# Modulation of a diffusion step in units of 1024 columns on one Trainium2 core

## The chip, the core and the metric

One core of one Trainium2 chip runs the whole program. The metric is the device time of one execution in microseconds; lower is better. The engines are TensorE (PE; PEld is its weight load), VectorE (DVE), ScalarE (ACT), GpSimd (POOL) and SyncE (SP), which here issues almost all DMAs, in the order of the program.

## The reference, cut to what matters

The model has two layers, 128 context and 256 latent tokens, and a width D of 1024. Each layer begins with a modulation that depends on nothing but two conditioning vectors (one for context, one for latent tokens):

```python
def adaln(cond, w, b):
    m = jax.nn.silu(cond) @ w + b          # w: (1024, 6 * 1024)
    return jnp.split(m[..., None, :], 6, axis=-1)
# shift1, scale1, gate1, shift2, scale2, gate2
h = layer_norm(x) * (1 + scale1) + shift1
...
x = layer_norm(alpha * x + gate1 * mix)
x = layer_norm(alpha * x + gate2 * peer(layer_norm(x) * (1 + scale2) + shift2))
```

So the modulation weights are 2 x 1024 x 6144 floats, 50 MB, each read once and multiplied with two vectors. `mix` is a token mixer (state-space scan, neighbourhood attention, grouped-query attention) behind one combined input projection; `peer` looks 16 experts per head and token up out of 16384 by two score lists of 128 keys.

## The kernel before, in words

**Weights.** Every weight goes through one ring of eight buffers `w` of 512 KB (`wst`, N_RAW = 8), filled by SyncE in program order; a load is issued once the buffer that was filled eight loads earlier has been read. A block of the input projection is split into a high and a low part (`split`, lines 218 to 225: ScalarE casts `uh`, VectorE or, for the first N_FIRST = 3 blocks, GpSimd subtracts to `ul`; three buffers of each), and multiplied in 24 matmuls of 384 columns (`proj3`, lines 361 to 371).

**Modulation.** `adaln_unit` (line 253) makes 256 columns of one of the six parts of one layer. It loads two `w` buffers, multiplies each of the eight k-slices with the conditioning `condT` (128 x 32, of which two columns are used), k-slice k in column group k % 4 of the array, so that PSUM holds four partial sums below each other (line 259). ScalarE copies them to `modp` (line 261). The second half of the unit, run when the next unit has begun, multiplies `modp` with a 0/1 table `sel` in two matmuls of two columns (line 265), which adds the four partial sums and puts the columns on partitions; two ScalarE operations add the bias and write `mcol` (line 268). There are 48 units, in the list `todo`.

```python
for k in range(KD):
    q = k % 4
    T.matmul(ps[32 * q:32 * q + 32, :256], condT[:, k, :], w[k], start=(k < 4), stop=(k >= 4), tile_position=(0, 32 * q))
...
for a in range(2):
    T.matmul(pt[:, 2 * a:2 * a + 2], mp[:, a * 128:(a + 1) * 128], sel, start=True, stop=True)
```

**Where the units run.** Eight run at the start (line 438): `cond_prep` makes `condT` and the bias columns `bmT`; then for each pair of k-slices two units (a shift and a scale) and behind them the transposes of the normalised tokens (line 441), modulated by ScalarE (line 444, `hraw`) and split into `hh` and `hl`. In the mixer, `blocks` (line 373) runs one unit behind every second weight block, up to N_FILL = (16, 8) by layer. At the third token tile of the output projection N_AD = 4 more run (line 1110; in layer 1 all that are left, two). In the routing of layer 0, `tick` (line 1187) runs one behind each of the query blocks 6 to 15. Routing is a loop over 16 query blocks of TensorE, each followed on VectorE by top-16 searches (`best`), with a long piece (`pairs`) behind blocks 7 and 15.

A tile scheduler orders the instructions of each engine at build time; engines then run them in that order and wait on semaphores.

Of the kernel before, what the change touches and what calls it, by code (L numbers as in the profile page):

```python
# [19 lines left out]
KD = 8  # L20
# [20 lines left out]
N_FILL = (16, 8)  # L41
N_AD = (4, 4)
# [11 lines left out]
R_AD = 4  # L54
# [55 lines left out]

CAND = []
# [44 lines left out]
def hybrid_step(ctx: ExitStack, tc: tile.TileContext, A, O):  # L156
# [71 lines left out]
    fill_ps, fill_n, first = [None], [0], [0]  # L228


    def cond_prep(sp, ps1):
        cond = mk(sp, [16, 128], "cond")
        dma(out=cond[0:8, :], in_=A["c_ctx"].rearrange("(k p) -> k p", p=128))
        dma(out=cond[8:16, :], in_=A["c"].rearrange("o (k p) -> (o k) p", p=128))
        V.memset(condT, 0.0)
        ps = mk(ps1, [128, 512], "pt")
        T.transpose(ps[:, :16], cond, ident[:16, :16])
        th = mk(sp, [128, 16], "cth")
        S.activation(th, ps[:, :16], AF.Tanh, scale=0.5)
        cc = mk(sp, [128, 16], "cc")  # L240
        S.activation(cc, ps[:, :16], AF.Copy, scale=0.5)
        V.scalar_tensor_tensor(condT[:, :, 0:2].rearrange("p k c -> p c k"), th.rearrange("p (c k) -> p c k", c=2), 1.0,
                               cc.rearrange("p (c k) -> p c k", c=2), op0=ALU.add, op1=ALU.mult)
        for l in range(DEPTH):
            bm = mk(sp, [48, 128], "bm", bufs=2)
            dma(out=bm, in_=A["b_mod"][l].rearrange("(k p) -> k p", p=128))
            ps = mk(ps1, [128, 512], "pt")
            T.transpose(ps[:, :48], bm, ident[:48, :48])
            V.tensor_copy(bmT[:, l], ps[:, :48])
            for part in (1, 4):  # L250
                V.tensor_scalar(bmT[:, l, part * KD:(part + 1) * KD], bmT[:, l, part * KD:(part + 1) * KD], 1.0, None, op0=ALU.add)

    def adaln_unit(l, part, hb, ps1, tags):

        w = load_k(A["w_mod"][l, part * 4 + hb])
        ps = mk(ps1, [128, 512], tags[0])
        for k in range(KD):
            q = k % 4
            T.matmul(ps[32 * q:32 * q + 32, :256], condT[:, k, :], w[k], start=(k < 4), stop=(k >= 4), tile_position=(0, 32 * q))
        mp = mk(outer, [128, 256], "modp", bufs=2)  # L260
        S.copy(mp, ps[:, :256])
        yield
        pt = mk(ps1, [128, 512], tags[1])
        for a in range(2):
            T.matmul(pt[:, 2 * a:2 * a + 2], mp[:, a * 128:(a + 1) * 128], sel, start=True, stop=True)
        c = part * KD + 2 * hb
        for a in range(2):
            S.activation(mcol[:, l, part, 2 * hb + a, :], pt[:, 2 * a:2 * a + 2], AF.Identity, bias=bmT[:, l, c + a:c + a + 1])

    todo = []  # L270
    for l, ps in ((0, (0, 1)), (0, (2,)), (0, (3, 4)), (1, (0, 1)), (0, (5,)), (1, (2,)), (1, (3, 4)), (1, (5,))):
        todo += [(l, part, hb) for hb in range(4) for part in ps]
    begun = []

    def adaln(n, ps1, tags, flush=False):

        for _ in range(min(n, len(todo))):
            u = adaln_unit(*todo.pop(0), ps1, tags)
# [94 lines left out]
    def blocks(src, b0, n):  # L373

        for j in range(n):
            yield load_w(src[b0 + j])
            if j % 2 and fill_n[0] > 0:
# [40 lines left out]
    def mixer(l, stack, right, ps1):  # L418
# [4 lines left out]
        with ExitStack() as sc0:  # L423
# [6 lines left out]
            if l == 0:  # L430
# [19 lines left out]
        fill_ps[0], fill_n[0], first[0] = ps1, N_FILL[l], N_FIRST  # L450
# [573 lines left out]
    def peer(l, mg, right, mps, ps1):  # L1024
# [162 lines left out]
        def tick(b):  # L1187
            u_steps(U_R.get(b, 0))
            if l == 0 and b >= N_WQ + R_AD:
# [124 lines left out]
def blocked(inputs):  # L1314
# [15 lines left out]
    d["w_mod"] = cut(d["w_mod"], 4, 256)  # L1330
# [28 lines left out]
```

## Time and profile before

| | us |
|---|---|
| three runs, median | 2998.48 |
| lowest, highest | 2995.82, 3007.12 |
| the profiled execution | 3004.09 |
| its span | 3002.3 |
| PE busy in the span | 2855.6 (95%) |
| DVE busy | 2309.1 (77%) |
| ACT busy | 1396.8 (47%) |

By time the span is: start until about 50 us; mixer of layer 0 until 486; output projection until 543; routing until 715; gate table and experts until about 1545; the same for layer 1, mixer until 1988, routing until 2192, experts until the end. Busy time is a share of the span only; whether a piece of work costs time is read from the waits of its stage.

### The profile page before, as it was taken

Reading aid. Unit: us, or ns where it says so; the run is one execution under the profiler, and the core shown is the slowest. Engines: PE = TensorE matmul, PEld = TensorE weight load, DVE = VectorE, ACT = ScalarE, POOL = GpSimd, SP = SyncE. Lnnn points to the kernel's source line nnn. Section 1 sums busy time; section 2 is a strip of 40 time slices with the busy share of each in tenths; the row PEclk is TensorE's granted clock in tenths of the full one; section 3 lists DMA queues with packets and bytes.
Section 4 is the critical chain, followed back from the end, with each engine's and each line's share of the span. In section 5 each row is a group of like instructions: output and inputs, shape, how many; then the busy total and the mean of one; then the engine's idle time right before and its main releaser. Section 6 shows DMA issues by size and latency. Waiting matters only on the chain.

```text
span 3002.3 us, 48719 instructions
## 1 busy us (share of the span) xinstructions
PE 2855.6 (95%) x17953; PEld 2479.3 (83%) x17953; DVE 2309.1 (77%) x4888; ACT 1396.8 (47%) x2861; POOL 824.8 (27%) x566
## 2 busy tenths in 40 slices
PE   7999999999889999999969999999987999999996
PEld 5888889877779999998858888898876999999985
DVE  3645654599669999998976466547986999999988
ACT  4544543225754444444445455432178544444443
POOL 1000000002334455554540000000033444555554
PEclk9999999999889999999979999999999999999998
DMA  6454322565999999999934432233569999999994
GB/s 246 151 159 146 95 72 87 182 223 167 316 364 408 391 392 396 393 391 369 379 97 144 127 93 74 85 111 113 156 217 371 418 395 392 394 391 394 393 364 166
DMA packets 299328, 767.09 MB, mean 256 GB/s; under 512 B 42770, under 2 KB 113874, under 8 KB 299090
## 3 DMA queue, kind: packets, MB, share of 16 engines
q1 hardware_dynamic: 225362, 495.51, 46.2%
q0 software_dynamic: 73728, 268.47, 23.5%
q8 instruction: 141, 2.31, 0.3%
q14 instruction: 97, 0.79, 0.1%
HBM read 726.92 MB, written 36.96 MB: 254 GB/s over the span
## 4 chain that ended last, share of the span: by engine, by line
PE 74%; DVE 11%; DMA 6%; ACT 4%; issue 4%; POOL 1%; SPq 0%; POOLq 0%; ACTq 0%; DVEq 0%
PE hp L1167 6%; PE out L1243 6%; PE hp L1169 6%; PE out L1245 6%; PE hp L1168 6%; PE out L1244 6%; PE pp L368 5%; PE pp L369 5%; PE pp L370 5%; PE hp L1164 4%; DMA w<-in_peer_uT 3%; PE pp L947 2%; ACT ol L1004 2%; DVE vl L224 2%; DVE tn L1073 2%
## 5 line engine op out<-in xcount | busy, mean ns | idle before, releaser
L1057 POOL DMA_INDIRECT prow<-in_peer_u,ei x256 | 363.1, 1418 | 763.1 <-DVE prow L1062 523.5
L1068 POOL DMA_INDIRECT prow<-in_peer_v,ei x256 | 382.4, 1494 | 350.1 <-DVE tn L1073 308.6
L222 ACT CAST vh<-w 128x1024 fp32r<-128x1024 f32 x256 | 268.9, 1050 | 367.9 <-issue 285.8
L1167 PE MATMUL hp<-hh,uh 128*128 128x256 f32 x1488 | 434.7, 292 | 0.0
L1169 PE MATMUL hp<-hh,ul 128*128 128x256 f32 x1488 | 417.1, 280 | 0.0
L1168 PE MATMUL hp<-hl,uh 128*128 128x256 f32 x1488 | 416.5, 280 | 0.0
L1245 PE MATMUL out<-vh,al 128*128 128x512 f32 x1024 | 400.0, 393 | 3.6 <-DVE al L1230 3.6
L1244 PE MATMUL out<-vl,ah 128*128 128x512 f32 x1024 | 397.5, 390 | 2.9 <-DVE vl L224 2.9
L1243 PE MATMUL out<-vh,ah 128*128 128x512 f32 x1024 | 392.9, 400 | 1.4 <-ACT ah L1228 1.4
L224 DVE TENSOR_TENSOR vl<-w,vh 128x1024 fp32r<-128x1024 f32 x256 | 315.8, 1234 | 62.7 <-ACT vh L222 44.0
L1073 DVE SCALAR_TENSOR_TENSOR tn<-prow,pact,tn 128x1024 f32<-128x1024 f32 x254 | 325.4, 1281 | 2.7
L1155 ACT CAST uh<-w 128x1024 fp32r<-128x1024 f32 x186 | 195.2, 1050 | 252.6 <-PE hp L1168 240.6
L368 PE MATMUL pp<-hh,uh 128*128 128x384 f32 (+1 forms) x848 | 297.9, 351 | 7.5 <-ACT hh L344 3.8
L1062 DVE SCALAR_TENSOR_TENSOR prow<-prow,tn 128x1024 f32<-128x1024 f32 x256 | 302.4, 1219 | 0.1
L1164 PE MATMUL hp<-hs,w 128*128 128x256 f32 x1120 | 270.1, 398 | 30.0 <-DMA w<-in_peer_uT 30.0
L370 PE MATMUL pp<-hh,ul 128*128 128x384 f32 (+1 forms) x848 | 297.0, 350 | 1.4 <-POOL ul L224 1.4
L369 PE MATMUL pp<-hl,uh 128*128 128x384 f32 (+1 forms) x848 | 294.8, 348 | 0.2 <-DVE xr L494 0.2
L1167 PEld LDWEIGHTS hp<-hh,uh 128*128 128x128 f32 x1488 | 281.1, 189 | 0.0
L1169 PEld LDWEIGHTS hp<-hh,ul 128*128 128x128 f32 x1488 | 281.1, 189 | 0.0
L1168 PEld LDWEIGHTS hp<-hl,uh 128*128 128x128 f32 x1488 | 281.1, 189 | 0.0
L224 DVE TENSOR_TENSOR ul<-w,uh 128x1024 fp32r<-128x1024 f32 x124 | 149.8, 1208 | 162.2 <-ACT uh L222 158.2
L1164 PEld LDWEIGHTS hp<-hs,w 128*128 128x128 f32 x1120 | 218.8, 200 | 63.4 <-DMA w<-in_peer_uT 33.1
(401 smaller groups left out, 5637.9 us busy)
## 6 DMA issues: line engine op xcount, KB each, us to landing
w<-in_peer_uT SPq DMA_DIRECT2D x256, 512.0 KB
w<-in_peer_v SPq DMA_DIRECT2D x256, 512.0 KB
w<-in_w_in SPq DMA_DIRECT2D x104, 512.0 KB
w<-in_w_mod SPq DMA_DIRECT2D x96, 512.0 KB
gd<-w SPq DMA_DIRECT2D x64, 512.0 KB
gt<-gd SPq DMA_DIRECT2D x64, 512.0 KB
w<-in_peer_wq SPq DMA_DIRECT2D x32, 512.0 KB
w<-in_w_branch SPq DMA_DIRECT2D x24, 512.0 KB
```

What stands on the lines that cost most here:

```text
L224: e.tensor_tensor(lo, src, hi.bitcast(F32), op=ALU.subtract)
L368: T.matmul(o, wh[:, k, :], hh[:, k, :], start=(k == 0), stop=False)
L369: T.matmul(o, wh[:, k, :], hl[:, k, :], start=False, stop=False)
L370: T.matmul(o, wl[:, k, :], hh[:, k, :], start=False, stop=(k == KD - 1))
L1073: V.scalar_tensor_tensor(acc, row, act[:, j:j + 1], acc, op0=ALU.mult, op1=ALU.add)
L1164: T.matmul(o, ut[0][:, k, :], hs[:, k, :], start=(k == 0), stop=(k == KD - 1))
L1167: T.matmul(o, uh[:, k, :], hh[:, k, :], start=(k == 0), stop=False)
L1168: T.matmul(o, uh[:, k, :], hl[:, k, :], start=False, stop=False)
L1169: T.matmul(o, ul[:, k, :], hh[:, k, :], start=False, stop=(k == KD - 1))
L1243: T.matmul(o, ah[:, ts], vh[:, ns], start=f, stop=False)
L1244: T.matmul(o, ah[:, ts], vl[:, ns], start=False, stop=False)
L1245: T.matmul(o, al[:, ts], vh[:, ns], start=False, stop=e)
```

## The change

A unit now makes 1024 columns. Its weights are eight loads, one for each k-slice, with 1024 columns each; every load is multiplied in four matmuls of 256 columns, column group q taking columns 256 q to 256 q + 255, and the eight k-slices add up in PSUM. So the copy `modp` holds finished sums, and two full transposes (128 x 128) put them on partitions; VectorE adds the bias. There are 12 units in place of 48: two at the start (the first half of shift and scale, then the second), five in the mixer of layer 0 behind every sixth block, one at its output projection, three in its routing (behind query blocks 9, 12 and 15), and one in the mixer of layer 1. `cond` and the bias come transposed from the host (128 rows of 64 and of 384 bytes), which drops three small transposes at the start.

```diff
-N_FILL = (16, 8)
-N_AD = (4, 4)
+N_FILL = (5, 2)
+FILL_BY = 6
+N_AD = (1, 1)
+UNITS = [((0, 0, 0, 4), (0, 1, 0, 4)), ((0, 0, 4, 4), (0, 1, 4, 4))]
+UNITS += [((l, part, 0, 8),) for l, part in ((0, 2), (0, 3), (0, 4), (1, 0), (1, 1), (0, 5), (1, 2), (1, 3), (1, 4), (1, 5))]
...
-    def adaln_unit(l, part, hb, ps1, tags):
-        w = load_k(A["w_mod"][l, part * 4 + hb])
+    def adaln_unit(u, ps1, tags):
         ps = mk(ps1, [128, 512], tags[0])
         for k in range(KD):
-            q = k % 4
-            T.matmul(ps[32 * q:32 * q + 32, :256], condT[:, k, :], w[k], start=(k < 4), stop=(k >= 4), tile_position=(0, 32 * q))
+            w = mk(wst, [128, RAWC], "w")
+            dma(out=w, in_=A["w_mod"][u, k])
+            for q in range(4):
+                T.matmul(ps[32 * q:32 * q + 32, :256], condT[:, k, :], w[:, q * 256:(q + 1) * 256], start=(k == 0), stop=(k == KD - 1), tile_position=(0, 32 * q))
         mp = mk(outer, [128, 256], "modp", bufs=2)
         S.copy(mp, ps[:, :256])
         yield
         pt = mk(ps1, [128, 512], tags[1])
         for a in range(2):
-            T.matmul(pt[:, 2 * a:2 * a + 2], mp[:, a * 128:(a + 1) * 128], sel, start=True, stop=True)
-        c = part * KD + 2 * hb
-        for a in range(2):
-            S.activation(mcol[:, l, part, 2 * hb + a, :], pt[:, 2 * a:2 * a + 2], AF.Identity, bias=bmT[:, l, c + a:c + a + 1])
+            T.transpose(pt[:, a * 128:(a + 1) * 128], mp[:, a * 128:(a + 1) * 128], ident)
+        pv = pt[:, :256].rearrange("p (a q m) -> p q a m", a=2, q=4)
+        j = 0
+        for l, part, k0, n in UNITS[u]:
+            for c in range(2):
+                V.tensor_tensor(mcol[:, l, part, k0:k0 + n, c].rearrange("p (q a) -> p q a", a=2), pv[:, j // 2:(j + n) // 2, :, c],
+                                bmT[:, l, part * KD + k0:part * KD + k0 + n].rearrange("p (q a) -> p q a", a=2), op=ALU.add)
+            j += n
...
             yield load_w(src[b0 + j])
-            if j % 2 and fill_n[0] > 0:
+            fill_at[0] += 1
+            if fill_n[0] > 0 and fill_at[0] % FILL_BY == 0:
                 fill_n[0] -= 1
                 adaln(1, fill_ps[0], ("pp", "pt"))
...
-                    if k % 2 == 0:
-                        adaln(2, ps1, ("pp", "pt"), True)
+                    if k % 4 == 0:
+                        adaln(1, ps1, ("pp", "pt"), True)
...
-            if l == 0 and b >= N_WQ + R_AD:
+            if l == 0 and b in (9, 12, 15):
                 adaln(1, pu, ("uT", "hp"), b == 15)
```

Three places show what moved. The first is TensorE at the start of the program, between the first modulation units and the transposes of the normalised tokens (`pp` and `pt` are PSUM tiles of a unit, `pa` those of the transposes). Before:

```order
L265 MATMUL pt_189<-cst_63,modp_172 128x2 x2
L259 MATMUL pp_178<-w_176,condT_73 32x256 x4
L265 MATMUL pt_194<-cst_63,modp_187 128x2 x2
L259 MATMUL pp_221<-w_217,condT_73 32x256 x4
L441 MATMUL pa_266<-cst_63,xn_117 128x128
L441 MATMUL pa_266<-cst_63,xn_131 128x128
L441 MATMUL pa_266<-cst_63,xn_145 128x128
L259 MATMUL pp_221<-w_219,condT_73 32x256 x4
L441 MATMUL pa_315<-cst_63,xn_117 128x128
L441 MATMUL pa_315<-cst_63,xn_131 128x128
L441 MATMUL pa_315<-cst_63,xn_145 128x128
L265 MATMUL pt_247<-cst_63,modp_230 128x2 x2
```

Now:

```order
L256 MATMUL pp_145<-w_188,condT_73 32x256 x4
L262 MATMUL pt_196<-cst_63,modp_194 128x128 x2
L256 MATMUL pp_239<-w_240,condT_73 32x256 x4
L442 MATMUL pa_230<-cst_63,xn_103 128x128
L442 MATMUL pa_230<-cst_63,xn_117 128x128
L442 MATMUL pa_230<-cst_63,xn_131 128x128
L256 MATMUL pp_239<-w_246,condT_73 32x256 x4
L442 MATMUL pa_297<-cst_63,xn_103 128x128
L442 MATMUL pa_297<-cst_63,xn_117 128x128
L442 MATMUL pa_297<-cst_63,xn_131 128x128
L256 MATMUL pp_239<-w_252,condT_73 32x256 x4
L442 MATMUL pa_306<-cst_63,xn_103 128x128
```

The small matmuls with `modp` stood behind every unit; now there is one pair of transposes behind 32 matmuls, and the token transposes alternate with single loads of the second unit.

The second is SyncE's queue in the mixer of layer 0, at the blocks of the neighbourhood keys and values (a `w_in` row is one block of the input projection). Before:

```order
L210 DMA w_1648<-in_w_in 128x1024
L210 DMA w_1680<-in_w_in 128x1024
L210 DMA w_1712<-in_w_mod 128x1024
L210 DMA w_1714<-in_w_mod 128x1024
L210 DMA w_1732<-in_w_in 128x1024
L210 DMA w_1764<-in_w_in 128x1024
L210 DMA w_1796<-in_w_mod 128x1024
L210 DMA w_1798<-in_w_mod 128x1024
```

Now:

```order
L213 DMA w_1626<-in_w_in 128x1024
L213 DMA w_1658<-in_w_in 128x1024
L254 DMA w_1691<-in_w_mod 128x1024
L254 DMA w_1697<-in_w_mod 128x1024
L254 DMA w_1703<-in_w_mod 128x1024
L254 DMA w_1709<-in_w_mod 128x1024
L254 DMA w_1715<-in_w_mod 128x1024
L254 DMA w_1721<-in_w_mod 128x1024
L254 DMA w_1727<-in_w_mod 128x1024
L254 DMA w_1733<-in_w_mod 128x1024
L725 DMA ck_2208<-in_cache_na_k 128x512
L727 DMA cv_2210<-in_cache_na_v 128x512
L213 DMA w_1746<-in_w_in 128x1024
```

Before, two modulation loads stood between pairs of blocks; now eight stand in one run, and the block behind them (`w_1746`) is the eighth load of the ring behind the first of them, so it takes the buffer of that first one.

The third is TensorE in the routing of layer 0 (`uT` is the PSUM tile of a unit, lines 915 and 947, now 916 and 948, are the query products of a block, 921 and 922 the key scores). Before, around blocks 6 and 7:

```order
L915 MATMUL pp_5589<-prow_4957,w_5587 128x128 x8
L947 MATMUL pp_5589<-hs_4729,w_5587 128x256 x8
L259 MATMUL uT_5868<-w_5864,condT_73 32x256 x4
L259 MATMUL uT_5868<-w_5866,condT_73 32x256
L921 MATMUL pn_5606<-gel_4753,qT_5607 128x128 x3
L259 MATMUL uT_5868<-w_5866,condT_73 32x256 x3
L265 MATMUL hp_5879<-cst_63,modp_5585 128x2 x2
L915 MATMUL pp_5886<-prow_4957,w_5884 128x128 x8
L947 MATMUL pp_5886<-hs_4729,w_5884 128x256 x8
L259 MATMUL uT_5933<-w_5929,condT_73 32x256 x4
L259 MATMUL uT_5933<-w_5931,condT_73 32x256
L921 MATMUL pn_5903<-gel_4760,qT_5904 128x128 x3
```

Now, around blocks 9 and 10:

```order
L948 MATMUL pp_5774<-hs_4631,w_5772 128x256 x8
L256 MATMUL uT_5817<-w_5818,condT_73 32x256 x4
L256 MATMUL uT_5817<-w_5824,condT_73 32x256
L922 MATMUL pn_5791<-gel_4662,qT_5792 128x128 x3
L256 MATMUL uT_5817<-w_5824,condT_73 32x256 x3
L256 MATMUL uT_5817<-w_5830,condT_73 32x256 x4
L256 MATMUL uT_5817<-w_5836,condT_73 32x256 x4
L256 MATMUL uT_5817<-w_5842,condT_73 32x256 x4
L256 MATMUL uT_5817<-w_5848,condT_73 32x256 x4
L256 MATMUL uT_5817<-w_5854,condT_73 32x256 x4
L256 MATMUL uT_5817<-w_5860,condT_73 32x256 x4
L262 MATMUL hp_6054<-cst_63,modp_5866 128x128 x2
L916 MATMUL pp_5870<-prow_4859,w_5868 128x128 x8
L948 MATMUL pp_5870<-hs_4631,w_5868 128x256 x8
```

Before, ten matmul groups of two loads followed ten blocks; now 32 matmuls follow blocks 9, 12 and 15, and blocks 6, 7 and 8 follow each other without any.

## Rows read from the trace of the kernel before

**Rows 1.** Page of the profile, part 1: busy time and share of each engine.
```profile
PE 2855.6 (95%) x17953; PEld 2479.3 (83%) x17953; DVE 2309.1 (77%) x4888; ACT 1396.8 (47%) x2861; POOL 824.8 (27%) x566
```

**Rows 2.** Chain that ended last, layer 0, second fill: start, us, what.
```profile
72.44 1.00 PE pp L259 x16
...
73.44 0.54 PE pt L265 x4
...
73.98 0.29 PE pp L368
...
74.80 0.18 PE pp L369
```

**Rows 3.** Groups of TensorE, 60 to 490 us (mixer of layer 0): busy, mean ns.
```profile
L259 PE MATMUL pp<-w,condT 128*32 128x256 f32 x256 | 19.0, 385 | 0.0
```

**Rows 4.** Line 259 in 1540 to 1720 us (mixer of layer 1).
```profile
L259 PE MATMUL pp<-w,condT x128: 379/379/569, 1564.5 to 1687.6; 128*32 128x256 f32 x128
```

**Rows 5.** Instructions in order of time, 0 to 75 us: start, us, what.
```profile
12.91 0.19 DVE L242 SCALAR_TENSOR_TENSOR condT<-cth,cc 128x16 f32<-128x16 f32 x1
...
24.64 0.90 PE L441 MATMUL pa<-cst,xn 128*128 128x128 f32 x3
...
24.79 0.37 ACT L261 COPY modp<-pp 128x256 f32<-128x256 f32 x1 [0.28 <-PE pp L259]
...
26.16 1.93 PE L259 MATMUL pp<-w,condT 128*32 128x256 f32 x16
...
29.94 1.26 ACT L444 ACTIVATE hraw<-pa,mcol 128x128 f32<-128x128 f32 x3
...
48.23 1.05 ACT L222 CAST uh<-w 128x1024 fp32r<-128x1024 f32 x1
...
49.36 7.35 POOL L224 TENSOR_TENSOR ul<-w,uh 128x1024 fp32r<-128x1024 f32 x3 [48.91 <-ACT uh L222]
...
51.78 0.69 PE L370 MATMUL pp<-hh,ul 128*128 128x384 f32 x1 [1.44 <-POOL ul L224]
```

**Rows 6.** Windows of 5 us from the start (last: clock, DMA share, GB/s).
```profile
15.00:20.00 5.00, 4.68 (x30) 2.34 (x26) 1.02 (x4) 2.12 (x5) 0.00 (x0) 1.00 1.03 420
```

**Rows 7.** Chain that ended last, 1515 to 1720 us: four loads of 64 KB.
```profile
1551.83 7.10 DMA xw<-in_state_ssd
```

**Rows 8.** Line 222, 50 to 480 us: what its engine waited for (us, times).
```profile
  PE pp L369: 78.9, 30
```

**Rows 9.** SyncE's queue in order of time: one load of 512 KB, alone.
```profile
237.10 0.33 SPq L210 DMA_DIRECT2D w<-in_w_branch  x1
```

**Rows 10.** Windows of 0.5 us behind it (clock, DMA share, GB/s).
```profile
240.00:240.50 0.50, 1.00 0.17 66
```

**Rows 11.** Page, part 5: the low part of a weight block.
```profile
L224 DVE TENSOR_TENSOR ul<-w,uh 128x1024 fp32r<-128x1024 f32 x124 | 149.8, 1208 | 162.2 <-ACT uh L222 158.2
```

**Rows 12.** Chain that ended last, 500 to 790 us.
```profile
537.51 5.46 DMA w<-in_peer_wq
...
573.72 3.46 PE pp L947 x16
...
579.85 3.46 PE pp L947 x16
...
597.28 0.98 PE uT L259 x10
...
605.57 0.98 PE uT L259 x10
```

**Rows 13.** TensorE in order of time, layer 1, after the output projection.
```profile
2035.86 1.09 PE L329 MATMUL pa<-cst,prow 128*128 128x128 f32 x8 [0.21 <-DVE prow L312]
```

**Rows 14.** VectorE in order of time, routing of layer 0.
```profile
599.67 0.49 DVE L870 MAX8 sv<-psc 128x8 f32<-128x128 f32 x2 [3.98 <-ACT psc L923]
...
710.33 0.24 DVE L977 SCALAR_TENSOR_TENSOR i<-i,ef 128x128 f32<-128x128 f32 x1
...
715.77 0.23 DVE L974 TENSOR_SCALAR i<-ef 128x128 f32<-128x128 f32 x1 [4.05 <-PE pp L979]
```

More of the change, by code (lines that the diff above doesn't have):

```diff
@@ L53 @@
 N_PSC = 8
-R_AD = 4
 CE_G = 0
@@ L227, in hybrid_step @@
     spool = [None]
-    fill_ps, fill_n, first = [None], [0], [0]
+    fill_ps, fill_n, fill_at, first = [None], [0], [0], [0]
     def cond_prep(sp, ps1):
-        cond = mk(sp, [16, 128], "cond")
-        dma(out=cond[0:8, :], in_=A["c_ctx"].rearrange("(k p) -> k p", p=128))
-        dma(out=cond[8:16, :], in_=A["c"].rearrange("o (k p) -> (o k) p", p=128))
+        cond = mk(sp, [128, 16], "cond")
+        dma(out=cond, in_=A["cond"])
+        dma(out=bmT, in_=A["b_mod"])
         V.memset(condT, 0.0)
-        ps = mk(ps1, [128, 512], "pt")
-        T.transpose(ps[:, :16], cond, ident[:16, :16])
@@ L238, in cond_prep @@
         th = mk(sp, [128, 16], "cth")
-        S.activation(th, ps[:, :16], AF.Tanh, scale=0.5)
+        S.activation(th, cond, AF.Tanh, scale=0.5)
         cc = mk(sp, [128, 16], "cc")
-        S.activation(cc, ps[:, :16], AF.Copy, scale=0.5)
+        S.activation(cc, cond, AF.Copy, scale=0.5)
         V.scalar_tensor_tensor(condT[:, :, 0:2].rearrange("p k c -> p c k"), th.rearrange("p (c k) -> p c k", c=2), 1.0,
                                cc.rearrange("p (c k) -> p c k", c=2), op0=ALU.add, op1=ALU.mult)
[L244 to L251, printed above, removed]
@@ L253, in adaln_unit @@
-    def adaln_unit(l, part, hb, ps1, tags):
-        w = load_k(A["w_mod"][l, part * 4 + hb])
+        for part in (1, 4):
+            b = bmT[:, :, part * KD:(part + 1) * KD]
+            V.tensor_scalar(b, b, 1.0, None, op0=ALU.add)
+    def adaln_unit(u, ps1, tags):
         ps = mk(ps1, [128, 512], tags[0])
         for k in range(KD):
-            q = k % 4
-            T.matmul(ps[32 * q:32 * q + 32, :256], condT[:, k, :], w[k], start=(k < 4), stop=(k >= 4), tile_position=(0, 32 * q))
+            w = mk(wst, [128, RAWC], "w")
+            dma(out=w, in_=A["w_mod"][u, k])
+            for q in range(4):
+                T.matmul(ps[32 * q:32 * q + 32, :256], condT[:, k, :], w[:, q * 256:(q + 1) * 256], start=(k == 0), stop=(k == KD - 1), tile_position=(0, 32 * q))
@@ L264, in adaln_unit @@
         for a in range(2):
-            T.matmul(pt[:, 2 * a:2 * a + 2], mp[:, a * 128:(a + 1) * 128], sel, start=True, stop=True)
-        c = part * KD + 2 * hb
-        for a in range(2):
-            S.activation(mcol[:, l, part, 2 * hb + a, :], pt[:, 2 * a:2 * a + 2], AF.Identity, bias=bmT[:, l, c + a:c + a + 1])
-    todo = []
-    for l, ps in ((0, (0, 1)), (0, (2,)), (0, (3, 4)), (1, (0, 1)), (0, (5,)), (1, (2,)), (1, (3, 4)), (1, (5,))):
-        todo += [(l, part, hb) for hb in range(4) for part in ps]
+            T.transpose(pt[:, a * 128:(a + 1) * 128], mp[:, a * 128:(a + 1) * 128], ident)
[6 more added lines that the diff above has]
+            j += n
+    todo = list(range(len(UNITS)))
     begun = []
@@ L277, in adaln @@
         for _ in range(min(n, len(todo))):
-            u = adaln_unit(*todo.pop(0), ps1, tags)
+            u = adaln_unit(todo.pop(0), ps1, tags)
             next(u)
@@ L449, in mixer @@
                 ln_mod_T(l, t, 0, 1, sp, mk(sp, [128, D], "xn", bufs=3), ps1, "pt", raw, lambda ks: parts(raw[:, ks], hh[:, ks, ts], hl[:, ks, ts], V if t == 2 else G))
-        fill_ps[0], fill_n[0], first[0] = ps1, N_FILL[l], N_FIRST
+        fill_ps[0], fill_n[0], fill_at[0], first[0] = ps1, N_FILL[l], 0, N_FIRST
         ysT = [mk(mo, [128, 4, NTOK], f"y{i}", dt=F32 if i else F32R) for i in range(3)]
@@ L1329, in blocked @@
     d["peer_wq"] = cut(d["peer_wq"], KD, 128)[:, :, 0]
-    d["w_mod"] = cut(d["w_mod"], 4, 256)
+    m = d["w_mod"].reshape(DEPTH, KD, 128, 6, KD, 128)
+    d["w_mod"] = np.stack([np.concatenate([m[l, :, :, part, k0:k0 + n].reshape(KD, 128, n * 128) for l, part, k0, n in u], axis=2) for u in UNITS])
+    d["b_mod"] = d["b_mod"].reshape(DEPTH, 48, 128).transpose(2, 0, 1)
+    d["cond"] = np.concatenate([d.pop("c_ctx").reshape(KD, 128), d.pop("c").reshape(KD, 128)]).T
     d["w_out"] = cut(d["w_out"], 4, 256)
```

## The prediction

> **What bounds the kernel now.** I first read the busy shares: TensorE is busy for 95% of the span [rows 1], so work taken from TensorE may count, but only where nothing else ends last. So I went through the chain that ended last, stage by stage, and asked at each modulation unit whether it stands in that chain. In the mixers it does: in the chain of layer 0 one unit is 1.00 us for its 8 matmuls (16 records), 0.54 us for the two small matmuls with `modp`, and the projection matmul behind it takes 0.29 us where its neighbours take 0.18 [rows 2]. So a unit costs 1.00 + 0.54 + 0.11 = 1.65 us of TensorE. The groups of TensorE show 256 records of line 259 in the mixer of layer 0, which is 16 units [rows 3], and 128 in that of layer 1, 8 units [rows 4]. The timeline of the start tells another story: there four things follow each other on different engines, and TensorE runs at about half its later speed, 8 matmuls in 1.93 us and three transposes in 0.90 [rows 5], although the granted clock reads 1.00 there [rows 6]; I call this half speed. The first sustained projection matmul comes at 51.78, behind the first subtraction of GpSimd [rows 5]. In the routing of layer 0 two chains run side by side, TensorE's blocks and VectorE's searches; VectorE's timeline shows which is later.
>
> **The matmuls with `condT`.** 48 x 8 before, 12 x 32 now: 384 of the same shape, four column groups at work in both orders. I take 0.125 us each (1.00 / 8) [rows 2], no change. What goes is the 96 small matmuls at 0.27 us and the turn to a 32-column array and back, 0.11 us, 48 times; what comes is 24 transposes, 0.30 us at half speed [rows 5], so about 0.15 at full. A new unit costs 4.0 + 0.3 + 0.1 = 4.4 us against 6.6 for the four that it replaces. ScalarE loses 36 copies and 96 small operations, VectorE gains 26 small additions of about 0.2 us (the nearest is the 0.19 of the `condT` operation [rows 5]); neither is the bound in the mixers, so nothing for both there.
>
> **The start.** `condT` is ready at 12.91 [rows 5] as before. The first unit needs 32 matmuls at 0.24, 7.7 us, with six transposes between (1.8) and about 0.5 of waiting for their inputs: 22.9. The copy (0.37, and 0.1 to start), two transposes (0.6) and four additions (0.8) bring the first modulation operation of ScalarE to 25.0. Its first bank is free after two of them, at 26.0 (the order interleaves the second unit with the transposes and `pa` has three banks). From there TensorE has four groups of three transposes and seven groups of four matmuls before it: 4 x 0.90 + 7 x 0.97 = 10.4, so 36.4. Copy 0.5, then the cast of the first block 1.05 [rows 5], then GpSimd's subtraction, a third of 7.35 [rows 5], and 0.2 between: 40.7 for the matmul that now stands at 51.78. I take back 0.5 because the last k-slice is modulated late. **Gain 10.6.** The loads do not set this: 16 x 0.524 MB and 2.2 MB ahead of them are 10.6 MB, at 420 GB/s [rows 6] 25 us. The bounds are 17, if the runs of matmuls without transposes between bring TensorE to full speed (its half of about 13 us would go), and 6, if the transposed `cond` and bias arrive late. They now come in 128 rows of 64 and 384 bytes; the nearest row is four loads of 64 KB in pieces of 256 bytes, which landed 7.10 us after the first issue [rows 7], against about 10 us in which `cond` may land here unnoticed. So I take no delay. The Trainium skill's page "DMA: Bandwidth & Descriptors", section "Specifications", speaks against this part of the change: it wants 512 bytes or more in a piece for full rate, below which the engine reads, modifies and writes. No run here shows that rate by itself; by that rule `condT` would come some us later and the sum would lose as much, up to the 5 that lie between my value and my lower bound.
>
> **Mixer of layer 0.** 16 units at 1.65 are 26.4; five new ones at 4.4 are 22.0: gain 4.4. The change adds a wait. Before, two loads of a unit stood between blocks, and the ring ran ahead: the casts of blocks waited for TensorE to free `uh`, 30 times, 78.9 us [rows 8], never for a load. Now a unit fills the ring, and the block behind it is loaded only when the unit's first four matmuls are done, 0.55 us into it. A lone load takes 3.1 us, from its issue at 237.10 [rows 9] to the end of its traffic in the window at 240.0 [rows 10]; with the cast (1.05) and the subtraction (1.21 [rows 11]) `ul` is ready 0.55 + 3.1 + 1.05 + 1.21 + 0.3 for the hand-overs = 6.2 us into the unit, whose work ends at 4.4 to 4.7, and one pair of matmuls (0.35) can go ahead. That leaves 1.3 us where the block follows at once (the third and fourth units), less where other work lies between (the first, before the small `dt` block; the second and fifth, among the scan and the attention). I take 3.6 for the five. **Gain 0.8**, between 4.4 and a loss of 10 (three loads in a row instead of one).
>
> **Output projections.** Layer 0: the four units wait for `peer_wq`, 5.46 us behind its issue [rows 12], and one and a half of them are done after that; the new unit is done before. **Gain 1.5** (0 to 3). Layer 1: two units go, but the transposes behind them already wait for VectorE, 0.21 us [rows 13]; without the units they wait longer. **Gain 0.**
>
> **Routing of layer 0.** Without a unit a block takes 579.85 - 573.72 = 6.13 us, with one 605.57 - 597.28 = 8.29 [rows 12]. Ten units cost 21.6; three new ones at 4.4 and 0.3 for the key scores that cut each in two cost 14.1: TensorE is through 7.5 us earlier. But VectorE is not: it waited for block 7 until 599.67, works without a pause from there, has its last input ready at 710.6, and waits then for TensorE until 715.77 [rows 14]. So 5.2 us can be had for nothing. Block 7 itself comes 1.9 us earlier (two units less before its scores, 2.6, but its scores now stand behind three query matmuls of block 8), and VectorE has six additions more, 1.2. **Gain 5.2 + 1.9 - 1.2 = 5.9** (2 to 7.5). Late next is VectorE.
>
> **Mixer of layer 1.** 8 units at 1.65 are 13.2, one at 4.4 remains, with 0.3 of waiting: **gain 8.5** (5 to 10). A unit and a half of work thus leaves layer 1 for places where it is covered or was already paid.
>
> **Sum.** 10.6 + 0.8 + 1.5 + 5.9 + 8.5 = 27.3 us. From the 3004.09 of the profiled execution that is 2976.8; that execution lies 5.6 above the median of 2998.48, so the forecast is 2971. Behind each of these places comes a stage that waits for it (projection, routing, gate table), so I carry the gains to the end. About 0.5%, 15 us, is what a measurement of this kernel can tell from no change.
>
> **The rivals.**
> *The ring runs dry.* If the load behind a unit is not alone but third in a row (2 x 1.3 us more), and TensorE falls to half speed in the wait (the first 24 matmuls behind it at 0.32 in place of 0.18 would cost 2 us), a unit pays 1.3 + 2.6 + 2 = 5.9 us, at six places 35. The gains without any waits are 31.2, so the kernel would be some 4 us slower, 3002; it is slower from 5.2 us a unit, and by more than 15 us from 7.7. For it speaks that eight loads really stand in one run; against it that the queue is nearly empty between loads in the mixers [rows 10]. Chance 0.10, of which 0.06 beyond 15 us.
> *The start alone moves.* If the small matmuls in the mixers were hidden, or the waits eat both mixers, what remains is the start and half of the routing, 10.6 + 3 = 14: 2985. For it speaks that the new waits are nearly as large as the gain in layer 0; against it, that the units stand in the chain [rows 2]. Chance 0.20.
> *The start at full speed.* Gain 17 in place of 10.6: 2965. For it speaks that runs of 16 or 20 matmuls now stand together; against it, that the start of the kernel is dense already and slow throughout [rows 5]. Chance 0.10.
>
> **How the numbers follow.** The forecast, 2971, has 0.60. Its own bounds: waits and start together 10 us worse, 8 better. The range for 8 in 10 runs from 2956 (the forecast's better end, 2963, less the 6.4 that a start at full speed adds, rounded down) to 2993 (the start alone at 2985, with the 8 us that the waits of layer 0 could cost above what they gain). Faster by over 0.5% (below 2983.5): 0.57 of the forecast, all of the full-speed start, 0.07 of the start alone, 0.74. Slower: 0.06. The same: 0.20.
>
> **What would show it.** The first sustained projection matmul near 41 us; 24 transposes where 96 small matmuls were; in the mixers 4.4 us from the first matmul of a unit to its last, and behind the third and fourth units a wait of 1 to 2 us for `uh` or `ul`; VectorE without its pause before the gate table; the mixer of layer 1 some 8 us shorter. Wrong would be: waits of over 4 us behind the units, a first projection after 45 us, or a mixer of layer 1 that is as long as before.

## The result, and the profile after

| | before | after |
|---|---|---|
| median of four runs each, us | 3002.28 | 2968.27 |
| lowest, highest | 2995.82, 3007.12 | 2966.07, 2972.18 |
| ratio, 95% interval | | 0.9889 (0.9865 to 0.9914) |
| the profiled execution | 3004.09 | 2967.48 |
| its span | 3002.3 | 2965.7 |

The change makes the kernel 1.1% faster, with an interval clear of 1; the forecast was 2971 in a range of 2956 to 2993. That the total came out does not yet mean that the working did. So I cut both executions at the same matmuls (the second record of line 370, the last product of the output projection, the first and the last query product behind it, the gate table's first product, the first and last expert output; in layer 1 the mixer is counted from the first record of line 370) and set the gain of each piece beside the term of the sum:

| stretch, us | before | after | gain | forecast |
|---|---|---|---|---|
| start | 52.9 | 36.2 | 16.7 | 10.6 |
| mixer of layer 0 | 483.1 | 476.6 | 6.5 | 0.8 |
| its output projection | 23.5 | 24.3 | -0.8 | 1.5 |
| query blocks of layer 0 | 104.1 | 99.3 | 4.8 | 5.9 with the next |
| from there to the gate table | 51.8 | 56.4 | -4.6 | |
| gate table of layer 0 | 157.0 | 153.9 | 3.1 | 0 |
| mixer of layer 1 | 475.8 | 463.1 | 12.7 | 8.5 |
| its output projection | 19.8 | 21.8 | -2.0 | 0 |
| all the rest | 1634.3 | 1634.1 | 0.2 | 0 |

Three terms came out too small, three too large. How far a stretch of one execution can be trusted: in the runs below that leave it alone, the gate table of layer 0 takes 154 to 157 us (157 before), the output projection of layer 0 21.5 to 23.8 (23.5 to 23.7 before), and the mixer of layer 1 459 to 463 (471 to 476 with the units of before). So the 3.1 may be nothing, the -0.8 belongs to this execution (the mean of eight other runs, 22.3, is a gain of 1.2), and 12.7 stands for anything from 8 to 17; the means of those runs, 473.4 and 460.2, differ by 13.2.

The page of the changed kernel, part 1; against [rows 1], TensorE has 47 us less work at the same share:

```profile
PE 2808.3 (95%) x17782; PEld 2449.6 (83%) x17782; DVE 2316.9 (78%) x4912; ACT 1370.9 (46%) x2729; POOL 819.0 (28%) x566
```

The start, instructions in order of time (start, us, what, idle before and releaser):

```profile
12.09 1.93 PE L256 MATMUL pp<-w,condT 128*32 128x256 f32 x16 [0.53 <-DVE condT L243]
...
16.63 2.35 PE L256 MATMUL pp<-w,condT 128*32 128x256 f32 x32
...
21.56 1.26 ACT L445 ACTIVATE hraw<-pa,mcol 128x128 f32<-128x128 f32 x3 [0.86 <-DVE mcol L268]
...
23.75 0.55 PE L442 MATMUL pa<-cst,xn 128*128 128x128 f32 x3
...
29.09 0.64 PE L256 MATMUL pp<-w,condT 128*32 128x256 f32 x8 [1.23 <-DMA w<-in_w_mod]
...
35.06 0.69 PE L370 MATMUL pp<-hh,ul 128*128 128x384 f32 x1 [0.47 <-POOL ul L227]
```

At 16.96 the granted clock rises, and TensorE goes faster: 16 matmuls in 2.35 us, a short wait included, where 8 took 1.93, three transposes in 0.55 where they took 0.90 [rows 5]. From about 27 us it waits for loads, and from 30.6 to 37.4 the granted clock is 0.50 again, so that the first projection matmuls run at half pace.

What TensorE waits for in the mixer of layer 0 (36 to 480 us; total, times, longest), the waits that the forecast placed behind the units:

```profile
PE pt L516 <- ACT dtT L512: 1.8, 1, 1.8
PE pp L368 <- ACT uh L225: 1.8, 3, 0.8
...
PE pp L370 <- DVE ul L227: 1.3, 2, 0.6
```

One whole unit in that mixer, then the block behind the third unit, in order of time:

```profile
167.90 3.66 PE L256 MATMUL pp<-w,condT 128*32 128x256 f32 x64
...
173.18 0.45 PE L368 MATMUL pp<-hh,uh 128*128 128x384 f32 x1 [0.83 <-ACT uh L225]
...
174.44 0.45 PE L370 MATMUL pp<-hh,ul 128*128 128x384 f32 x1 [0.64 <-DVE ul L227]
```

The routing of layer 0, chain that ended last:

```profile
585.46 0.61 PE uT L256 x8
586.09 4.18 DMA w<-in_w_mod
590.31 0.68 PE uT L256 x8
...
611.95 4.99 DMA w<-in_peer_wq
...
637.10 4.34 DMA w<-in_w_mod
...
674.14 1.39 issue
```

Each unit now waits for its last load, and one block behind a unit for its query weights. The lengths in the chain are whole loads, from issue to landing; TensorE itself works through most of that time and stands idle for less, as here:

```profile
590.31 0.64 PE L256 MATMUL uT<-w,condT 128*32 128x256 f32 x8 [0.28 <-DMA w<-in_w_mod]
```

All its waits from the first query product to the gate table come to 5.1 us, where the kernel before had none, and the granted clock is 0.50 for 3.4 us behind those at the second unit. VectorE, at the end of that routing:

```profile
693.18 0.23 DVE L975 TENSOR_SCALAR i<-ef 128x128 f32<-128x128 f32 x1 [5.72 <-PE pp L980]
```

Its wait for TensorE has grown from 4.05 us [rows 14] to 5.72. The output projection of layer 1, TensorE in order of time, and the windows behind it (TensorE busy, clock, DMA share, GB/s):

```profile
1997.78 1.94 PE L329 MATMUL pa<-cst,prow 128*128 128x128 f32 x8 [3.42 <-DVE prow L312]
...
1999.56 5.04 PE L916 MATMUL pt<-hs,w 128*128 128x128 f32 x26
```

```profile
1990.00:1994.00 4.00, 4.00 (x39) 1.00 0.04 17
...
1998.00:2002.00 4.00, 4.00 (x19) 0.50 0.00 0
```

The wait of 0.21 us [rows 13] has become 3.42, and from 1996.7, still within it, until 2003.5 the granted clock is 0.50: eight transposes take 1.94 us instead of 1.09.

### The profile page after: what moved, and what is told of

Its sections match the earlier page's. It is cut to its first block, busy times and chain, and to the rows that moved or that the text cites. A ratio compares the mean times of both kernels' runs of the same rounds, so it can differ in the third digit from the quotient of the medians.

```text
span 2965.7 us, 48246 instructions
## 1 busy us (share of the span) xinstructions
PE 2808.3 (95%) x17782; PEld 2449.6 (83%) x17782; DVE 2316.9 (78%) x4912; ACT 1370.9 (46%) x2729; POOL 819.0 (28%) x566
## 3 DMA queue, kind: packets, MB, share of 16 engines
q0 software_dynamic: 73728, 268.47, 23.8%
## 4 chain that ended last, share of the span: by engine, by line
PE 72%; DVE 12%; DMA 6%; ACT 4%; issue 4%; POOL 1%; SPq 0%; POOLq 0%; ACTq 0%; DVEq 0%
PE hp L1168 6%; PE out L1244 6%; PE out L1246 6%; PE hp L1170 6%; PE hp L1169 6%; PE out L1245 6%; PE pp L370 4%; PE pp L368 4%; PE pp L369 4%; PE hp L1165 3%; DMA w<-in_peer_uT 3%; PE pp L948 2%; ACT ol L1005 2%; DVE vl L227 2%; DVE tn L1074 2%
## 5 line engine op out<-in xcount | busy, mean ns | idle before, releaser
L351 POOL TENSOR_TENSOR res<-res,lg 128x384 f32<-128x384 f32 x6 | 8.8, 1461 | 897.5 <-ACT res L313 897.5
```

## The experiments

Expected texts name stretches of the table. A single time stands beside 2998.66 to 2999.64 us for the kernel before on the same chip; four runs of that kernel lay 11 us apart, so single times are read through their stretches.

### Start: the length of the runs

```diff
-                    if k % 2 == 0:
-                        adaln(2, ps1, ("pp", "pt"), True)
+                    if k % 4 == 0:
+                        adaln(4, ps1, ("pp", "pt"), True)
```

> The kernel before, with its eight units of 256 columns at the start run four and four (32 matmuls together) in place of two and two; everything else is as before. Theory 1, the run's length: 32 matmuls with little between them bring TensorE to full speed, 8 matmuls fall from 1.93 us to about 1.0, and the first sustained projection matmul comes at 36 to 42 us instead of 51.78; the kernel is some 10 us faster than before. Theory 2, the shape of the unit: what slowed the start were the small matmuls, copies and ScalarE operations of each small unit, of which none goes here; 8 matmuls stay at 1.93 us and the projection starts after 47 us; the time is that of before within 4 us.

2996.19 us; start 52.7. TensorE's rows, in order of time:

```profile
25.96 1.93 PE L259 MATMUL pp<-w,condT 128*32 128x256 f32 x16
28.38 1.01 PE L265 MATMUL pt<-cst,modp 128*128 128x2 f32 x4 [0.49 <-ACT modp L261]
```

The numbers are those of theory 2, but the run decides nothing: on every engine the scheduler put the instructions of the start in the same order as in the kernel before, and TensorE's 17953 records agree in order over the whole program. The small matmuls still stand behind every eighth large one, and no long run came about. This is a second execution of the kernel before, and shows only how far its stretches scatter (mixer of layer 1 471.0 and 475.8).

### Start: a warm TensorE

```diff
+        ps = mk(ps1, [128, 512], "pb")
+        for _ in range(28):
+            T.matmul(ps[:, :128], ones, ones, start=True, stop=True)
```

> The kernel before, with 28 matmuls of 128 columns of ones, whose result nobody reads, as TensorE's first work, while it waits for the first inputs. Theory 1, the clock: the start of the kernel before is long because TensorE works at half speed; warmed, 8 matmuls take 1.0 instead of 1.93 us, and the first sustained projection matmul comes at 38 to 44 us instead of 51.78. Theory 2, the chain: it is the hand-overs between TensorE, ScalarE and back, of which the small units need eight; then the projection starts at most 4 us earlier, at any speed of TensorE.

3000.32 us; start 52.5. TensorE in order of time, and windows of 5 us:

```profile
12.75 1.07 PE L262 MATMUL pp<-w,condT 128*32 128x256 f32 x16 [0.61 <-DVE condT L245]
...
25.73 1.93 PE L262 MATMUL pp<-w,condT 128*32 128x256 f32 x16
```

```profile
10.00:15.00 5.00, 2.08 (x22) 1.00 1.03 419
15.00:20.00 5.00, 4.57 (x26) 0.50 1.03 419
```

The first eight matmuls do run in 1.07 us, so the 1.93 of before was the 1.2 GHz level. But TensorE is idle for much of 10 to 15 us, the granted clock falls to 0.50, and the small units, though TensorE is busy for 4.0 to 4.7 of every 5 us up to 45, never bring it back. So neither theory's number was put to the test over the whole start. In the changed kernel the clock rises at 16.96, only 0.33 us into the 32 records in a row, so that run can hardly be what raised it; ahead of it stand 4.9 us of large matmuls and token transposes without the two-column matmuls, which in the kernel before come in from 17.96 on. That these hold the clock down is not shown.

### Routing: the loads spread over the blocks

The three units' 24 slices (load and four matmuls) two or three behind each block:

```diff
-            if l == 0 and b in (9, 12, 15):
-                adaln(1, pu, ("uT", "hp"), b == 15)
+            if l == 0 and b >= 6:
+                adaln_part(3 if b in (9, 11, 13, 15) else 2, pu, ("uT", "hp"))
+                if b == 15:
+                    finish()
```

> The changed kernel, with the 24 loads and matmul groups of the three units in the routing of layer 0 put two or three behind each of the query blocks 6 to 15, in place of eight behind blocks 9, 12 and 15. Theory 1, the ring: the last load of a unit takes the buffer of the block ahead of it and so lands late, which costs TensorE about 6 us of idle time and 2 us of slow clock; without it the query blocks end 7 to 8 us earlier, VectorE waits at the end for less than 2 us (8.9 now), and the kernel takes about 2960. Theory 2, VectorE: its searches with the six additions are the bound, and the routing becomes shorter by less than 3 us, 2965 or more.

2959.18 us, but not by the routing, which is 5.2 us longer: query blocks 102.3 (99.3), and 58.6 behind them (56.4). Groups of TensorE in this stretch (here, then in the changed kernel; busy, mean ns, idle before):

```profile
L256 PE MATMUL uT<-w,condT 128*32 128x256 f32 x192 | 18.8, 389 | 0.0
```

```profile
L256 PE MATMUL uT<-w,condT 128*32 128x256 f32 x192 | 13.4, 384 | 1.4 <-DMA w<-in_w_mod 1.4
```

The wait for the loads is gone, and the same 96 matmuls are busy for 5.4 us more (4.0 from each record to the next, waits left out and the units' transposes counted): the key scores cut them into 21 runs of 3 to 7 where the changed kernel has three of 5 and three of 27. How much of this is the turn of the array was not measured by itself. Behind the last block TensorE also waits six times 0.47 us for `gel` and once 1.07, 4.0 us in all; the next two runs explain these. Both theories fall short: the wait is real, but this edit pays for it with something as dear. The length of a run is itself a price that my sum had only in the 0.11 us per unit.

### Routing: buffers of their own

The units stay whole; the last four loads of each go to four more buffers:

```diff
-            w = mk(wst, [128, RAWC], "w")
+            w = mk(extra[0] if extra[0] is not None and k >= KD - 4 else wst, [128, RAWC], "w")
...
+            extra[0] = pool(sc2, "wx", bufs=4)
```

> The changed kernel; in the routing of layer 0 alone, the last four loads of each unit go into four buffers of their own, so that neither a unit nor the block behind it waits for the ring. The units stay whole. Theory 1, the ring: the three waits for a unit's last load and the one for the query weights, with the slow clock behind one of them, are 7.3 us of TensorE in the routing; the stretch from the first query product after the output projection to the gate table's first product falls from 155.7 to 148 to 150 us, and what VectorE waits for at its end from 5.7 to under 2. Theory 2: TensorE has other waits in their place; 153 us or more.

2970.58 us. Query blocks 93.9, 5.4 less, so the waits were the ring's; but the stretch behind them is 70.1 in place of 56.4, and the two together, 164.0, miss the 148 to 150 of theory 1. The chain there, a product of TensorE, and VectorE:

```profile
605.66 3.15 PE uT L256 x54
...
661.39 9.45 issue
670.84 26.07 PE hp L1168 x112
```

```profile
640.88 3.72 PE L1168 MATMUL hp<-hs,w 128*128 128x256 f32 x16 [0.47 <-ACT gel L1175]
```

```profile
670.59 0.15 DVE L268 TENSOR_TENSOR mcol<-hp,bmT 128x8 f32<-128x8 f32 x1
```

The units no longer wait (27 matmuls in 3.15 us). Instead the expert products (`hp`), of which 14 stand behind the last block, wait 0.47 us each, five times, for ScalarE to empty the one bank left to them, then stop for 9.45 us and go on when VectorE has made the units' bias additions. Before the change ScalarE made these at once; now they are queued on VectorE behind the long piece `pairs`, and the transposes of two units hold two of the three banks `hp` from 631.6 on. In the changed kernel only the last unit's are left, in one bank, and the same shows as 1.39 us of "issue". This gave a new theory for the 4.6 us lost behind the query blocks.

### Routing: the bank

```diff
+        if tags[0] == "uT":
+            mt = mk(mtp[0], [128, 256], "modt", bufs=3)
+            S.copy(mt, pt[:, :256])
+            pt = mt
         pv = pt[:, :256].rearrange(...
```

> The changed kernel; in the routing of layer 0 ScalarE copies the two transposes of a unit out of PSUM (0.4 us), and VectorE adds the bias from that copy. Theory 1, the bank: the last units' additions stand behind VectorE's long piece and hold two of the three PSUM banks through which TensorE's expert products rotate; with the copy those products run without waits, and the stretch from the last query product to the gate table's first product falls from 56.4 to 52 or 53 us (51.8 before the change), the query blocks staying at 99. Theory 2: the products wait for their weights or for the activation, and the stretch stays above 55 us.

> The run with four buffers of their own for the units' loads, and this copy as well. Theory 1: both waits are real and independent; query blocks 94 us, the stretch behind them 52 to 53 (70.1 without the copy), so that the gate table is reached 8 to 10 us earlier than in the changed kernel, less what VectorE then lacks (it is ready some 8 us before TensorE now); the kernel takes 2956 to 2962. Theory 2: VectorE is the next bound there, and of the 9 us less than 4 are left.

Alone 2965.2 us: query blocks 98.2, behind them 55.5, VectorE's wait 3.83. In the chain the 14 products now stand in one piece, without a wait:

```profile
641.06 48.35 PE hp L1172 x224
```

So the bank was the cause of that wait. But the stretch misses the 52 or 53 of theory 1 and stays above 55 as in theory 2, though not for its reason: the last unit's late load lies in it too (TensorE is idle for 1.22 and 0.49 us there). With both edits, 2962.06: query blocks 93.9, 54.1 behind them instead of 70.1, together 148.0 against 155.7 and 155.9 before the change, and TensorE is idle for 0.1 us in all of it. So of the 4.6 us lost behind the query blocks 2.3 are waits; the other 2.3 are the last unit itself, which stands in that stretch and is now four times as large. VectorE passes the same place (line 975, here 981) without a wait:

```profile
688.36 0.22 DVE L981 TENSOR_SCALAR i<-ef 128x128 f32<-128x128 f32 x1
```

So both waits are shown, and VectorE is now the later one there: TensorE waits for it twice, 0.60 and 0.58 us. How much of the 7.7 us it keeps is not settled. Three to six are left at the end of the gate table (query blocks to the end of the gate table 306.4 us; 309.6 to 312.7 in the changed kernel and in the runs that leave this part alone or only copy); theory 2 wanted less than 4.

### Mixers: the loads spread over the blocks

Two slices behind each of 20 blocks in layer 0 and of 4 in layer 1, the sums in the bank `pb`:

```diff
-            if fill_n[0] > 0 and fill_at[0] % FILL_BY == 0:
+            if fill_n[0] > 0 and fill_at[0] >= FILL_AT:
                 fill_n[0] -= 1
-                adaln(1, fill_ps[0], ("pp", "pt"))
+                adaln_part(2, fill_ps[0], ("pb", "pt"))
```

> The changed kernel, with the 40 loads and matmul groups of the five units in the mixer of layer 0 put two behind each of 20 blocks (from the fifth on), and those of the one unit in the mixer of layer 1 two behind each of four blocks; the sums stand in the otherwise idle PSUM bank of the branches. Theory 1, the ring: the block behind eight loads in a row comes late; the waits of 0.27, 1.81, 1.47, 1.35 and 0.70 us behind the units in layer 0 and 0.85 in layer 1 go, 4 to 6 us in all. Theory 2: these waits belong to the places (the small block, the scan, the attention) and not to the loads; less than 1.5 us is gained.

2962.7 us; mixer of layer 0 477.7 (474.9 to 479.0 in the runs that leave it alone), of layer 1 457.4. What TensorE waits for in the mixer of layer 0, and the group of the unit's matmuls in it (20.6 us in the changed kernel, counted alike):

```profile
PE pt L763 <- DMA bt<-in_na_rpb: 1.9, 3, 0.8
PE pt L685 <- ACT tv L682: 0.6, 1, 0.6
PE pp L390 <- DVE hl L366: 0.5, 1, 0.5
```

```profile
L256 PE MATMUL pb<-w,condT 128*32 128x256 f32 x320 | 25.3, 397 | 0.0
```

The waits for `uh`, `ul` and `dtT` (4.9 us) are gone, so they came from the loads: theory 1 of their cause. Its gain is not to be seen: the 160 matmuls are busy for 4.7 us more, 3.0 from each record to the next, as in the routing, and the rest is within the scatter. In layer 1 the mixer is 1.6 to 5.7 us shorter than in the runs that leave it alone, but the stretch ahead of it, from the last expert output, takes 28.1 us where all others take 25.6, so next to nothing is gained there either.

### Shape or place

The kernel before, its small units four at a time at the places of the change:

```diff
-N_FILL = (16, 8)
+N_FILL = (5, 1)
+FILL_BY = 6
...
-                adaln(1, fill_ps[0], ("pp", "pt"))
+                adaln(4, fill_ps[0], ("pp", "pt"))
...
-            if l == 0 and b >= N_WQ + R_AD:
-                adaln(1, pu, ("uT", "hp"), b == 15)
+            if l == 0 and b in (9, 12, 15):
+                adaln(4, pu, ("uT", "hp"), b == 15)
```

> The kernel before with its units of 256 columns, four at a time, at the places of the change: 20 in the mixer of layer 0 behind every sixth block, 4 at its output projection, 12 in its routing behind blocks 9, 12 and 15, 4 in the mixer of layer 1. Theory 1, the shape: only what a unit costs counts; the mixer of layer 0 gets longer by four small units, from 483 to 487 to 493 us, that of layer 1 shorter by four, from 476 to 467 to 471, and the kernel takes 2990 to 3005. Theory 2, the places: fewer interruptions give the gain; the mixer of layer 0 takes 480 or less although it holds four units more, and the kernel 2985 or less.

3030.16 us: slower than both kernels and outside both theories. Start 51.8, mixer of layer 0 522.7, of layer 1 460.5. TensorE's waits at 280 to 345 us:

```profile
PE pt L414 <- DVE smr L410: 11.8, 5, 2.7
PE pt L414 <- DVE p L411: 4.6, 3, 2.8
```

In layer 0 this build orders TensorE differently in the attention, so that it has nothing to put between the softmax steps (16.4 us of waits, and the clock falls behind them); that is no price of a unit, and layer 0 says nothing here. Layer 1 has no such waits, and there four small units together (5.8 us of TensorE in that mixer, from each record to the next; 13.2 for the eight scattered ones of before, 3.9 for the one large one) are as good as the large one within the scatter (460.5, where theory 1 had 467 to 471). So the place in layer 1, four units fewer and one interruption in place of eight, carries most of its 12.7; the shape is worth about 1.9 us for 1024 columns, from this one place.

### Output projection of layer 1: what the wait costs

Seven matmuls that nobody reads, in the wait of 3.42 us:

```diff
+                if l == 1:
+                    ps = mk(ps1, [128, 512], "pp")
+                    for _ in range(7):
+                        T.matmul(ps[:, :256], ident, tn[:, :256], start=True, stop=True)
```

> The changed kernel, with seven matmuls of 256 columns (3.0 us together), whose result nobody reads, put into the 3.42 us wait of TensorE behind the output projection of layer 1. Theory 1, the clock: the wait lets TensorE fall to 1.2 GHz; with the filler the eight transposes behind it take 1.1 us instead of 1.94 and the 26 query matmuls 3.2 instead of 5.04, the granted clock there reads 1.00, and that place is passed 2.0 to 2.6 us earlier. Theory 2: the rows are slow for another reason (loads, PSUM); no row gets shorter, and the place is passed at the same time or up to 0.5 us later.

2960.94 us. TensorE in order of time:

```profile
1987.95 3.19 PE L1116 MATMUL pp<-tn,cst 128*128 128x256 f32 x14
1991.54 1.06 PE L329 MATMUL pa<-cst,prow 128*128 128x128 f32 x8 [0.40 <-DVE prow L312]
1993.32 3.39 PE L916 MATMUL pt<-hs,w 128*128 128x128 f32 x28 [0.72 <-ACT hs L334]
```

Theory 1: 1.06 instead of 1.94 us, 3.39 for 28 records instead of 5.04 for 26; the place takes 20.0 instead of 21.8 us (21.6 to 21.9 in the other runs that leave it alone), 1.8 less (2.0 to 2.6 expected). The wait cost its own time and then 1.8 of slow clock; idle work in it is enough to keep TensorE at 2.4 GHz.

The other way to fill it is the unit from the mixer (`N_FILL = (5, 0)`):

> The changed kernel with the one unit of the mixer of layer 1 moved to the output projection of that layer, where TensorE waits 3.42 us and is slow behind it. Theory 1: the mixer gets 4.9 us shorter (463.1 to about 458), the place (21.8 us from the last product of the output projection to the first query product of block 2) about 1.7 longer, since unit and load wait take the place of the wait and the slow clock; net 3 us faster. Theory 2: the unit's eight loads hold up the query weights for longer than the wait they fill; the place takes 27 us or more and nothing is gained.

2963.23 us: mixer 456.9, the place 22.6; 479.5 together, against 484.9 in the changed kernel and 481.0 to 482.2 in the other runs that leave both alone, so 1.5 to 5.4 us are gained. TensorE there:

```profile
1985.70 0.64 PE L256 MATMUL pp<-w,condT 128*32 128x256 f32 x8 [0.36 <-DMA w<-in_w_mod]
1988.55 0.71 PE L916 MATMUL pt<-prow,w 128*128 128x128 f32 x4 [2.21 <-DMA w<-in_peer_wq]
```

The unit costs the place 0.8 us instead of the 1.7 expected: theory 1.

### Together

> The run before this one with the last unit moved to the output projection of layer 1 as well. If both act, some 9 us in the routing of layer 0 and 3 us in layer 1 come off the changed kernel: 2952 to 2958, 1.4 to 1.7 per cent below the kernel before. If VectorE bounds the routing: 2960 to 2965.

Four runs: median 2954.34 us (2949.94 to 2956.72) against 2998.97 (seven runs), ratio 0.9859 (0.984 to 0.9878). This lies in the range for both edits acting, and below the one for a routing bound by VectorE. It beats both kernels as the medians stand, but its interval overlaps that of the change, 0.9865 to 0.9914. The stretches are as in the single edits: query blocks 93.9, 54.1 behind them, mixer of layer 1 454.4, the place behind it 22.4.

## Why the prediction was right, and where it was not

**The matmuls with `condT`: right.** 32 matmuls take 3.66 us, 0.114 each where I took 0.125; with 0.44 for the transposes a unit costs 4.1, not 4.4. (VectorE's additions are 28, not 26.)

**The start: the mechanism right, the size off.** The term "7.7 us" for 32 matmuls at 0.24 failed: TensorE reached full speed in the fourth slice, at 16.96. The first sustained projection matmul came at 35.06, not 40.7, the rival "start at full speed" to a third of a microsecond (16.7 of 17); but the start was not at full speed throughout, so that its number fits is luck. "The loads do not set this" failed too: the last slices of the second unit wait for them until 30.3 us. The 25 us were right for the bytes at 420 GB/s, but the loads moved at 208 and 374 GB/s in the first two stretches of 5 us; from 10 to 35 us the DMA share stays at 1.02 or 1.03. How much of the 16.7 the clock gives was not isolated: both runs meant for it left it open. Nothing in the trace shows `condT` late: `cond` lands 7.4 us after its issue, and `condT` is computed at 11.86 instead of 12.91 [rows 5], which is 1.05 of the 16.7. What the Trainium skill's page "DMA: Bandwidth & Descriptors", section "Specifications", says of pieces below 512 bytes, and would have cost up to 5 us by my reckoning, is not to be seen here: no run shows that rate by itself.

**Mixer of layer 0: the terms right, one missing.** Forecast were 4.4 of work and 3.6 of waits; the units' matmuls, from each record to the next without waits, went from 25.1 to 21.5 us and TensorE's idle time from 4.8 to 9.2, with 1.47 and 1.35 us behind the third and fourth units where 1.3 was worked out. What the sum lacked is that all other work there got 7.2 us faster. Windows at the granted clock of 0.50, before and after:

```profile
138.10:148.30 10.20, 10.20 (x46) 0.50 0.21 78
175.70:182.40 6.70, 6.70 (x29) 0.50 0.23 73
```

```profile
153.50:156.90 3.40, 3.40 (x12) 0.50 0.36 137
```

Some 17 us at 1.2 GHz became 3.4, which returns half the difference, 6.8 us; in the seven other runs with these units in this mixer 3.4 to 10.3 us are left, so 3.4 to 6.8 come back. The first stretch before stood behind a wait of 2.1 us in the scan, which the new order cut to two of 0.3:

```profile
PE pa L628 <- DVE w L619: 2.1, 1, 2.1
```

That this wait was the cause is not shown. In the scan of layer 1, where the kernel before has the same wait, the slow stretch behind it was 10.2, 6.8 and 0 us long in three runs with the units of before, and the changed kernel has 10.1 behind a wait of 0.3:

```profile
1641.80:1651.90 10.10, 10.10 (x41) 0.50 0.15 52
```

In this pair of executions 16.7 us at half speed in that scan became 10.1, worth 3.3 of the 4.2 that the 8.5 lacks. The waits behind units did not bring TensorE down in the mixers, and they were the 1.3 of the forecast, not the 3.9 of the rival "the ring runs dry", which had neither its wait nor its clock. (Its 24 matmuls at 0.14 more are 3.4 us, not 2, so it was priced too low.)

**Routing: wrong.** The work was right: without the waits TensorE reaches the gate table 7.9 us earlier than before the change, where 7.5 were forecast. What the sum put at nothing is the waits, 7.7 us. "Three new ones at 4.4" left out that a unit of eight loads needs the whole ring, so that its last load takes the buffer of the block just ahead: 5.4 us of waits and slow clock in the query blocks and 0.9 behind them (shown by the extra buffers). "VectorE has six additions more, 1.2" priced the additions and not what they hold up: queued behind 32 us of VectorE's work, the last ones kept a PSUM bank from TensorE, which cost 1.4 us (shown by the copy). Together they ate the 5.9, and VectorE's wait did not go. VectorE's own part held: it is done 150.3 us behind the first query product instead of 152.2, where 0.7 was forecast and a pause of 1.37 us at 666.01 had been overlooked.

**Output projections.** In layer 1 "they wait longer" was right, but that this costs anything was missing: 2.0 us, of which unread matmuls in the wait brought back 1.8. In layer 0 a wait for the query weights stands behind the unit, where I had none, and my 1.5 came out as -0.8:

```profile
520.88 0.71 PE L916 MATMUL pt<-prow,w 128*128 128x128 f32 x4 [2.76 <-DMA w<-in_peer_wq]
```

The eight other runs give 1.2 there on average, so the 1.5 was not far off.

So the total was right by luck: in these two executions errors of 10 us (5.7 in the routing, 4.3 at the output projections) met 16 the other way (6.1 at the start, 5.7 and 4.2 in the mixers). The gain was underestimated, 27.3 against 34.0 between the medians; the time came within 3 us of the forecast also because the kernel before stands at 3002.28 here, and stood at 2998.48, the median of three runs, when the forecast was made.

## What to carry to other kernels

Large units of work on one engine pay by fewer small operations and fewer interruptions, but a unit as large as the ring of buffers makes its own last load and the next block wait; spreading it out again removes the waits and loses the long runs. When a step moves to another engine, ask what stands ahead of it in that queue and what memory its inputs hold meanwhile. When a wait of TensorE grows to some microseconds, look at the granted clock behind it as well: here a wait of 3.42 us brought 1.8 us of slow work with it. And read one stretch in several executions before explaining a few microseconds of it.

## What the runs showed of the hardware

The granted clock was at 0.50 (the 1.2 GHz level) for 6.8 us from within the wait of 3.42 us on; 3.2 us of useless matmuls in that wait prevented it. Behind a wait of 2.1 us in the scan it was at 0.50 for 10.2 us in layer 0, but in layer 1 behind the same wait for 10.2, 6.8 and 0 us in three runs. In the first 50 us the column of the clock cannot be read before its first change: the kernel before shows 1.00 there with matmuls at the pace that reads 0.50 in the warmed run. And 96 matmuls in runs of 3 to 7 were busy for 18.8 us where the same 96, most of them in runs of 27, took 13.4, waits not counted.
